# A trunk of eight token tiles on one core: the last pass of three stages in a fixed order, with the next stage's operands made between the finishing steps

## The chip, the core and the metric

One core of a Trainium2 chip runs the whole kernel in one launch. TensorE multiplies, VectorE and ScalarE finish and split results, GpSimd raises one small power per token tile and issues some transfers, and SyncE issues most transfers. The metric is the device time of one launch in microseconds, lower is better. In the profile TensorE is PE, VectorE is DVE, ScalarE is ACT, GpSimd is POOL and SyncE is SP.

## What is computed

1024 tokens of 1024 channels go through two layers, in float32:

```python
for i in range(2):
    hn = rmsnorm(h, norm_mix_g[i])
    h = h + (s5_mixer(hn, ...) if i == 0 else shortconv_mixer(hn, ...))
    h = h + swiglu_ffn(rmsnorm(h, norm_ffn_g[i]), ffn_w_in[i], ffn_w_out[i])
    gate = sigmoid(rmsnorm(h, norm_ple_g[i]) @ ple_w_gate[i])
    h = h + gate * (p[i] @ ple_w_up[i])
return rmsnorm(h, final_norm_g)
```

`s5_mixer` ends in a product with `w_glu` whose one half gates the other; `shortconv_mixer` begins with a product with `conv_w_in` and ends in one with `conv_w_out`; `swiglu_ffn` has a product into 2816 gated channels and one back.

## The kernel before

A float32 product is made of three TensorE passes over a high part and a low part (`split`: ScalarE copies the high part at line 87, VectorE subtracts the rest at line 88; `mm3`: lines 122 to 124). The tokens lie in eight tiles of 128, taken in the order `ORDER` = 0, 4, 1, 5, 2, 6, 3, 7.

The stages alternate between two forms. In the token form (`glu`, `ffn_out`, `ple`, `conv_out`) a tile's matmuls are followed by its finishing operations: a sigmoid where there is a gate, the addition into `h`, and a sum of squares by ScalarE (`square`, line 139). In the channel form (`ffn_in`, `conv_in`) the weights are stationary and all tokens stream past. It uses a scheme that makes a 2 x 2 block product with seven products instead of eight (`block_product`), for which sums and differences of weight blocks (`weights_set`, lines 275 to 283) and of token blocks are needed.

Three times a token stage is followed by a channel stage: `glu` before `ffn_in(0)`, `ple(0)` before `conv_in`, `conv_out` before `ffn_in(1)`. In the last pass over the tiles of these three, `h` becomes complete. Tiles q and q+4 make pair q. `norm_pair(q)` normalizes both (`normed`: the sum of squares at line 146, a power on GpSimd at line 148, the scaling to `xn` at line 173), transposes them on TensorE into four blocks (line 181: `p11`, `p21` from the first tile, `p12`, `p22` from the second), and makes the seven token operands with `put` (a `split`) and the differences T1 to T4 (lines 221 to 232). Operand 0 needs `p11` alone, operand 1 is T2, which needs `p12` and `p22`. `spill` stores `h` by a transfer issued from GpSimd.

Code order is not instruction order here. The framework's scheduler orders the instructions of each engine when the kernel is built, by priority and by its own estimate of times; `first()` raises the priority of the finishing operations and of `normed`. On the chip each engine then runs its list in that order. Buffers come from pools: the temporaries `upt`, `sgg`, `junk`, `b12` and T1 to T4 share five buffers of one tag in the three stages here.

Of the kernel before, what the change touches and what calls it, by code (L numbers as in the profile page):

```python
# [9 lines left out]
F32 = mybir.dt.float32  # L10
F32R = mybir.dt.float32r
# [12 lines left out]
def trunk(  # L24
# [102 lines left out]
    squares = {}  # L127

    def first():
        return tc.high_priority(offset=100)  # L130

    def square(t, cs):
# [5 lines left out]
        ms = squares["ms"][:, t, len(got):len(got) + 1]  # L138
# [3 lines left out]
    def norm_stat(t):  # L142
        ms, *more = squares.pop(t)
        V.tensor_scalar(ms, ms, EPS, None, ALU.add)
# [6 lines left out]
    def t2_tile(name, dt=F32, n=512):  # L151
        return t2.tile([P, n], dt, name=name, tag="t2")
# [54 lines left out]
    def norm_pair(q, gb):  # L207
        t0, t1 = q, q + HT
        halves = 2 if q == HT - 1 else 1
        x0, x1 = normed(t0, gb, halves), normed(t1, gb, halves)  # L210

        def put(c, src):
            split(moving_part(c, 0, q), moving_part(c, 1, q), by_kt(src))

        p11, p12, p22 = transposed(x0, 0), transposed(x1, 0), transposed(x1, 1)
        p21 = transposed(x0, 1, mm)
        put(0, p11)
        b12 = t2_tile("b12")
        A.copy(b12, p12)
        T1 = t2_tile("T1")  # L220
        V.tensor_tensor(T1, b12, p11, ALU.subtract)
        T2 = t2_tile("T2")
        V.tensor_tensor(T2, p22, T1, ALU.subtract)
        put(1, T2)
        put(2, T1)
        put(3, p21)
        T3 = t2_tile("T3")
        V.tensor_tensor(T3, p22, b12, ALU.subtract)
        put(4, T3)
        put(5, p22)  # L230
        T4 = t2_tile("T4")
        V.tensor_tensor(T4, p21, T2, ALU.subtract)
        put(6, T4)

# [23 lines left out]
    def weights_set(src_a, src_b):  # L258
# [15 lines left out]
        s3 = s_tile()  # L274
        V.tensor_tensor(s3, a11, a21, ALU.subtract)
        V.tensor_tensor(a21, a21, a22, ALU.add)
        s2 = s_tile()
        V.tensor_tensor(s2, a21, a11, ALU.subtract)
        ws2 = operand(s2)
        ws1 = operand(a21)  # L280
        w12 = operand(a12)
        ws3 = operand(s3)
        V.tensor_tensor(s2, a12, s2, ALU.subtract)
        return [w11, ws2, ws1, w12, ws3, operand(s2), operand(a22)]
# [131 lines left out]
    def ple(l, units, post):  # L416
# [683 lines left out]
```

## Time and profile before

| What | Value |
|---|---|
| median of 3 runs | 2356.54 us (2355.79 to 2357.86) |
| the profiled execution | 2359.43 us, of which the span is 2357.5 us |
| busy: PE, DVE, ACT, POOL | 2247.0, 1331.9, 765.5, 163.1 us |
| mean granted TensorE clock | 0.981 |
| waits of PE for the scaled tile `xn`, in the whole run | 36.0 us, 5 waits, the longest 10.7 us |
| last pass of `glu`, `ple(0)`, `conv_out` up to the first product of the next stage | 358.5 to 420.6, 1158.1 to 1225.6, 1507.9 to 1571.3 us |

The span runs from the first to the last instruction; 1.9 us of the launch lie outside it. The profiled execution is 2.9 us above the median of the runs. Busy time of PE is modelled for pipelined matmuls, so the waits say more than the 95%. In a timeline row the columns are start, duration, engine, line, operation, output<-inputs with their shapes, count, and in brackets the engine's idle time just before with what ended it.

### The profile page before, as it was taken

How to read it: one execution, taken by the hardware profiler on the slowest of the kernel's cores; microseconds unless marked ns; L12 is line 12 of the kernel's file. 1: busy time of each engine (PE TensorE's matmuls, PEld its weight loads, DVE VectorE, ACT ScalarE, POOL GpSimd, SP SyncE). 2: the span in 40 equal slices, each digit the busy share in tenths (PEclk: the TensorE clock that was granted, in tenths of full speed). 3: DMA queues.
4: the chain of work that ended last, by engine and by line, in shares of the span. 5: the costliest groups of instructions: out<-in, count | busy, mean ns of one | idle time of the engine just before them, and what ended most of it. 6: DMA issues, size and time to landing. Idle time of an engine off the chain costs nothing.

```text
span 2357.5 us, 27090 instructions
## 1 busy us (share of the span) xinstructions
PE 2247.0 (95%) x10253; PEld 1835.7 (78%) x10253; DVE 1331.9 (56%) x2246; ACT 765.5 (32%) x1449; POOL 163.1 (7%) x268
## 2 busy tenths in 40 slices
PE   6888999899999999999979999989999999999998
PEld 4776887788888878878858888768888888788787
DVE  7785326866666642125488776487666666121454
ACT  6554223433333320013343332153333333000232
POOL 2110001000000000000000000010000001000000
PEclk8999999999999999999989999999999999999999
DMA  7555202333333364333232225434333335543333
GB/s 246 141 135 148 69 1 89 105 112 112 111 114 110 107 241 149 118 127 114 70 129 81 90 92 179 159 125 125 108 108 107 111 113 172 212 139 107 108 109 110
DMA packets 212978, 288.87 MB, mean 123 GB/s; under 512 B 21360, under 2 KB 152432, under 8 KB 212848
## 3 DMA queue, kind: packets, MB, share of 16 engines
q1 hardware_dynamic: 191520, 212.63, 29.0%
q0 software_dynamic: 20928, 74.47, 10.2%
q8 instruction: 80, 1.31, 0.2%
q14 instruction: 50, 0.41, 0.1%
q10 hardware_dynamic: 400, 0.04, 0.0%
HBM read 190.93 MB, written 79.69 MB: 115 GB/s over the span
## 4 chain that ended last, share of the span: by engine, by line
PE 85%; DMA 6%; DVE 5%; ACT 1%; SPq 1%; issue 1%; POOL 0%; DVEq 0%; POOLq 0%; ACTq 0%
PE psmm L122 27%; PE psmm L124 27%; PE psmm L123 27%; DMA ch<-hid 2%; PE pstr L181 1%; DMA raw<-in_ffn_w_out_dram 1%; DMA tw<-tmp 1%; DVE W L575 1%; DVE gv L925 1%; DMA h<-hd 1%; DVE tmp L575 1%; DVE ulow L88 1%; DVE uhigh L88 1%; PE pstr L874 0%; DVE raw L575 0%
## 5 line engine op out<-in xcount | busy, mean ns | idle before, releaser
L122 PE MATMUL psmm<-ulow,ws 128*128 128x512 f32 x896 | 351.1, 393 | 1.6 <-ACT s L301 1.6
L123 PE MATMUL psmm<-ulow,ws 128*128 128x512 f32 x896 | 350.6, 391 | 0.0
L124 PE MATMUL psmm<-ulow,ws 128*128 128x512 f32 x896 | 350.4, 391 | 0.0
L124 PE MATMUL psmm<-uhigh,ws 128*128 128x512 f32 x672 | 265.3, 395 | 0.0
L122 PE MATMUL psmm<-uhigh,ws 128*128 128x512 f32 x672 | 265.1, 394 | 0.0
L123 PE MATMUL psmm<-uhigh,ws 128*128 128x512 f32 x672 | 264.9, 394 | 0.0
L360 DVE TENSOR_TENSOR h<-psmm,h 128x512 f32<-128x512 f32 x128 | 88.0, 690 | 276.6 <-PE psmm L124 276.6
L88 DVE TENSOR_TENSOR ws<-raw,ws 128x512 fp32r<-128x512 f32 x224 | 153.6, 688 | 117.8 <-ACT ws L87 117.4
L87 ACT CAST ws<-raw 128x512 fp32r<-128x512 f32 x224 | 137.5, 619 | 213.0 <-PE psmm L124 211.2
L122 PEld LDWEIGHTS psmm<-ulow,ws 128*128 128x128 f32 x896 | 169.4, 189 | 39.5 <-ACT s L301 2.9
L123 PEld LDWEIGHTS psmm<-ulow,ws 128*128 128x128 f32 x896 | 169.4, 189 | 36.2
L124 PEld LDWEIGHTS psmm<-ulow,ws 128*128 128x128 f32 x896 | 169.2, 189 | 36.2
L87 ACT CAST ws<-st 128x512 fp32r<-128x512 f32 x168 | 104.0, 620 | 204.4 <-PE psmm L124 189.5
L123 PEld LDWEIGHTS psmm<-uhigh,ws 128*128 128x128 f32 x672 | 126.1, 188 | 30.3
L124 PEld LDWEIGHTS psmm<-uhigh,ws 128*128 128x128 f32 x672 | 126.1, 188 | 30.3
L122 PEld LDWEIGHTS psmm<-uhigh,ws 128*128 128x128 f32 x672 | 126.1, 188 | 29.1
L323 POOL DMA_DIRECT2D hid<-hs x104 | 78.2, 755 | 903.4 <-DVE hs L88 895.4
L122 PE MATMUL psmm<-ulow,ch 128*128 128x512 f32 x320 | 128.4, 401 | 10.8 <-DMA ch<-hid 10.8
L139 ACT ACTIVATE junk<-h 128x512 bf16<-128x512 f32 (+1 forms) x113 | 64.0, 567 | 204.0 <-DVE h L360 104.0
L87 ACT CAST uhigh<-raw 128x1024 fp32r<-128x1024 f32 x36 | 37.2, 1049 | 278.9 <-PE psmm L124 136.7
L123 PE MATMUL psmm<-ulow,ch 128*128 128x512 f32 x320 | 127.6, 399 | 0.0
L124 PE MATMUL psmm<-ulow,ch 128*128 128x512 f32 x320 | 127.5, 398 | 0.0
(240 smaller groups left out, 4238.5 us busy)
## 6 DMA issues: line engine op xcount, KB each, us to landing
hid<-hs POOLq DMA_DIRECT2D x104, 512.0 KB, 4.3
ch<-hid SPq DMA_DIRECT2D x96, 512.0 KB, 3.7
raw<-in_ffn_w_in_dram SPq DMA_DIRECT2D x88, 512.0 KB, 4.4
raw<-in_ffn_w_out_dram SPq DMA_DIRECT2D x44, 512.0 KB, 3.6
hd<-h POOLq DMA_DIRECT2D x24, 512.0 KB, 3.0
h<-hd SPq DMA_DIRECT2D x24, 512.0 KB, 8.7
raw<-in_conv_w_in_dram SPq DMA_DIRECT2D x24, 512.0 KB, 4.0
up<-ev SPq DMA_DIRECT2D x32, 256.0 KB, 3.2
```

Of the source, the lines that this page charges most:

```text
L87: A.copy(hi, src)
L88: V.tensor_tensor(lo, src, hi.bitcast(F32), ALU.subtract)
L122: PE.matmul(ps, ahi, bhi, start=start, stop=False, skip_group_check=more)
L123: PE.matmul(ps, ahi, blo, start=False, stop=False, skip_group_check=more)
L124: PE.matmul(ps, alo, bhi, start=False, stop=stop, skip_group_check=more)
L139: A.activation(junk[:, cs], h[t][:, cs], AF.Square, scale=1.0 / math.sqrt(D), accum_out=ms)
L181: PE.transpose(pt[:, c * P:(c + 1) * P], xn[:, kt * P:(kt + 1) * P], ident)
L323: nc.gpsimd.dma_start(out=hid[ht // 4][half * HT:(half + 1) * HT, :, ht % 4].rearrange("t p l j -> p t l j"), in_=hs.bitcast(F32))
L360: V.tensor_tensor(h[t][:, cs], ps[nb], h[t][:, cs], ALU.add)
L575: V.tensor_tensor(o, a, b, op)
L925: V.tensor_tensor_scan(gv[:, g, 1:P], dec, sv[:, g, 1:P], 0.0, ALU.mult, ALU.add)
```

## The change

Three things change in the three stages. First, the last pass is written as one loop, `last_pass`, and every TensorE, VectorE and ScalarE instruction in it is chained to the one traced before it on the same engine (`lane`), so that these three engines run in the written order. The written order is, for each tile: its matmuls; with every second tile the 16 transposes of the pair before; then the finishing operations with the pair's steps (`pair_steps`, eleven of them) put in between, one after the addition, one after the squares, one after the sum of squares, and all that are left after `xn`. For the last pair, the first tile is transposed behind the last matmuls, the second when its `xn` is there. Second, the sums and differences of the first weight set of the next stage are held behind the last `xn` on VectorE. Third, the temporaries have their own buffers: `ta`, `tb`, `tc` for the differences, and two buffers instead of five for the rest.

Two things come with it. `conv_out` gets its own loop, in which both halves of a tile are added after all of its matmuls. And in `ple(1)`, which does not use `last_pass`, the two halves of the last tile, which before took one load of `upt`, now each load their own.

```diff
+    def lane():
+        traced = tc.nc.cur_bb.bb.instructions
+        n = len(traced)
+        yield
+        for ins in list(traced[n:]):
+            if ins.engine not in (PE.engine, V.engine, A.engine):
+                continue
+            if ins.engine in lane_ends:
+                tc.add_manual_dep(ins, lane_ends[ins.engine], ..., reason="lane")
+            lane_ends[ins.engine] = ins.name
...
+        return [plain(0, (0, 0)), both(copied, combine("T1", "tb", "b12", (0, 0))), combine("T2", "tc", (1, 1), "T1"),
+                lambda: put(1, tmp["T2"]), lambda: put(2, tmp["T1"]), combine("T4", "tb", (0, 1), "T2"),
+                plain(3, (0, 1)), combine("T3", "tc", (1, 1), "b12"), lambda: put(4, tmp["T3"]), plain(5, (1, 1)),
+                lambda: put(6, tmp["T4"])]
...
+    def last_pass(gb, run):
+        ...
+        with lane():
+            for i, t in enumerate(ORDER):
+                finish, cs = run(t)
+                if i in (2, 4, 6):
+                    q = i // 2 - 1
+                    p = pair_parts(q, {0: xs[q], 1: xs[q + HT]}, [((0, 0), tr), ((1, 0), tr), ((1, 1), tr), ((0, 1), mm)])
+                    todo.extend(pair_steps(q, p))
+                if i == T - 1:
+                    p = pair_parts(HT - 1, {0: xs[HT - 1]}, [((0, 0), mm), ((0, 1), mm)])
+                    steps = pair_steps(HT - 1, p)
+                    todo.insert(0, steps.pop(0))
+                if t in squares:
+                    stat_ahead(t)
+                finish()
+                do(1)
+                square(t, cs)
+                do(1)
+                rs = norm_stat(t, summed=True)
+                do(1)
+                xs[t] = xn = raw_tile(name="xn")
+                halves = 2 if i == T - 1 else 1
+                for c in range(halves):
+                    hs = slice(c * D // halves, (c + 1) * D // halves)
+                    ins = V.scalar_tensor_tensor(xn[:, hs], h[t][:, hs], rs, gb[:, hs], ALU.mult, ALU.mult)
+                spill(t)
+                if i < T - 1:
+                    do(3 if i % 2 else 99)
+            ends[:] = [ins.ins]
+            do(99)
+            p.update(pair_parts(HT - 1, {1: xs[T - 1]}, [((1, 0), tr), ((1, 1), tr)]))
+            todo.extend(steps)
+            do(99)
...
         w11 = operand(a11)
+        with tc.issue_after(ends.pop()) if ends else nullcontext():
             s3 = s_tile()
...
-                upt = t2_tile("upt")
-                nc.sync.dma_start(out=upt, in_=updram[l][:, t, cs])
...
+            def run(t, c0=0, c1=512):
+                hc = slice(nb * 512 + c0, nb * 512 + c1)
+                upt = t2_tile("upt")[:, 0:c1 - c0]
+                nc.sync.dma_start(out=upt, in_=updram[l][:, t, hc])
...
+            if nb == 1 and post is None:
+                last_pass(gb, run)
+                break
```

How the built lists differ is shown at three places, before first and then changed. In a row, `T_...` is a difference, `ws` a weight operand, `ulow` and `uhigh` the room of the token operands, `w_...` the weights of the token stage.

TensorE, last pass of `ple(0)`, around the transposes of the second pair. Before, the eight transposes of its second tile stand 32 matmuls behind the eight of its first:

```order
L124 MATMUL psmm<-w_8491,ulow 128x512
L181 MATMUL pstr<-ident,xn 128x128 x4
L181 MATMUL psmm<-ident,xn 128x128 x4
L122 MATMUL psmm<-w_8380,ulow 128x512
...
L123 MATMUL psmm<-w_8417,ulow 128x512
L181 MATMUL pstr<-ident,xn 128x128 x8
L124 MATMUL psmm<-w_8417,ulow 128x512
```

Changed:

```order
L124 MATMUL psmm<-w_8490,ulow 128x512
L208 MATMUL pstr<-ident,xn 128x128 x12
L208 MATMUL psmm<-ident,xn 128x128 x4
L122 MATMUL psmm<-w_8379,ulow 128x512
L123 MATMUL psmm<-w_8379,ulow 128x512
```

All 16 now stand together, directly behind the matmuls of the pair's following tile, and that tile's successor stands behind them.

VectorE, end of the last pass of `glu`, from the third pair's differences to the last `xn` and a little beyond. Before:

```order
L275 TENSOR_TENSOR st<-raw 128x512
L88 TENSOR_TENSOR ulow<-T_3550,ulow 128x4x128
L502 TENSOR_TENSOR sgg<-psmm,sgg 128x256
L88 TENSOR_TENSOR uhigh<-T_3558,uhigh 128x4x128
L88 TENSOR_TENSOR uhigh<-pstr,uhigh 128x4x128
L88 TENSOR_TENSOR uhigh<-T_3564,uhigh 128x4x128
L276 TENSOR_TENSOR raw<-raw 128x512
L503 TENSOR_TENSOR h<-sgg,h 128x256
L278 TENSOR_TENSOR st<-raw 128x512
L146 TENSOR_TENSOR ms<-ms 128x1
L173 SCALAR_TENSOR_TENSOR xn<-h,rs,gb 128x512 x2
L88 TENSOR_TENSOR ws<-raw,ws 128x512
```

Changed:

```order
L88 TENSOR_TENSOR uhigh<-T_3567,uhigh 128x4x128
L163 TENSOR_SCALAR ms<-ms 128x1
L165 TENSOR_TENSOR ms<-ms 128x1 x2
L595 TENSOR_TENSOR sgg<-psmm,sgg 128x256
L596 TENSOR_TENSOR h<-sgg,h 128x256
L88 TENSOR_TENSOR ulow<-psmm,ulow 128x4x128
L173 TENSOR_TENSOR ms<-ms 128x1
L303 SCALAR_TENSOR_TENSOR xn<-h,rs,gb 128x512 x2
L355 TENSOR_TENSOR st<-raw 128x512
L356 TENSOR_TENSOR raw<-raw 128x512
L88 TENSOR_TENSOR ws<-raw,ws 128x512
L358 TENSOR_TENSOR st<-raw 128x512
```

The three weight sums (lines 275, 276, 278, now 355, 356, 358) moved behind the last `xn`; the finishing of the last tile (lines 595, 596) stands behind the last step of the third pair, as every second tile's does behind its pair. From the last `xn` to the low half of the last pair's operand 1 twelve rows stand in between.

SyncE, the last loads and stores of the kernel, in `ple(1)`. Before:

```order
L424 DMA upt_16880<-up1_97 128x512 [waits DMAHW2_49,DVE_49]
L244 DMA out_0_dram<-xn_16874 128x512 [waits DMAHW3_49,DVE_49]
L244 DMA out_0_dram<-xn_16877 128x512 [waits DMAHW4_49,DVE_49]
L244 DMA out_0_dram<-xn_16947 128x512 [waits DMAHW5_49,DVE_49]
L244 DMA out_0_dram<-xn_16950 128x512 [waits DMAHW6_49,DVE_49]
```

Changed:

```order
L506 DMA upt_16877<-up1_97 128x256 [waits DMAHW2_49,DVE_49]
L323 DMA out_0_dram<-xn_16871 128x512 [waits DMAHW3_49,DVE_49]
L323 DMA out_0_dram<-xn_16874 128x512 [waits DMAHW4_49,DVE_49]
L506 DMA upt_16909<-up1_97 128x256 [waits DMAHW5_49,DVE_49]
L323 DMA out_0_dram<-xn_16946 128x512 [waits DMAHW6_49,DVE_49]
L323 DMA out_0_dram<-xn_16949 128x512 [waits DMAHW7_49,DVE_49]
```

The second half's load has become a transfer of its own, behind two stores, and it waits for VectorE, whose addition of the first half gives its buffer free.

More of the change, by code (lines that the diff above doesn't have):

```diff
@@ new lines, in trunk, with do @@
+    ends = []
+    def last_pass(gb, run):
+        xs, todo = {}, []
+        def do(n):
+            for _ in range(min(n, len(todo))):
+                todo.pop(0)()
+        with lane():
[10 more added lines that the diff above has]
+                if t in squares:
+                    stat_ahead(t)
+                finish()
[17 more added lines that the diff above has]
+            do(99)
+        lane_ends.clear()
@@ L503, in glu @@
                     V.tensor_tensor(h[t][:, cs], sg, h[t][:, cs], ALU.add)
+                return finish, cs
+            if nb == 3:
+                last_pass(gb, run)
+                break
+            for t in ORDER:
+                finish, _ = run(t)
+                with first():
+                    finish()
                     square(t, cs)
-                if nb == 3:
-                    post(t)
     def conv_in(cvq):
```

197 lines of the change are left out of this document (115 added, 82 removed).

## The prediction

> **What bounds the kernel now.** First the chain of waits on the page:
>
> ```profile
> PE 85%; DMA 6%; DVE 5%; ACT 1%; SPq 1%; issue 1%; POOL 0%; DVEq 0%; POOLq 0%; ACTq 0%
> ```
>
> The chain is TensorE (PE) for 85%: what the change can move is time in which PE waits. So next the waits of PE in the three last passes, from the first matmul of the pass to the first product of the next stage (`glu`, `ple(0)`, `conv_out`):
>
> ```profile
> PE pstr L181 <- DVE xn L173: 10.4, 1, 10.4
> PE pstr L181 <- DVE xn L173: 14.8, 3, 10.4
> PE pstr L181 <- DVE xn L173: 10.7, 1, 10.7
> ```
>
> Nearly all that PE waits there is for the scaled tile `xn`, 35.9 us in all. Then the windows of the three passes, and behind them of the next stages' first 168 matmuls (stretch, its length, busy us and instructions of PE, PEld, DVE, ACT and POOL, granted clock, share and GB/s of the DMA):
>
> ```profile
> 358.50:420.60 62.10, 51.68 (x258) 43.42 (x256) 42.84 (x77) 24.40 (x58) 9.07 (x16) 0.94 0.26 94
> 1158.10:1225.60 67.50, 52.66 (x258) 43.62 (x256) 47.33 (x77) 26.93 (x56) 9.10 (x17) 0.90 0.31 109
> 1507.90:1571.30 63.40, 52.69 (x257) 43.44 (x256) 46.44 (x82) 26.02 (x60) 9.64 (x16) 0.94 0.38 133
> 420.60:461.90 41.30, 40.62 (x170) 32.53 (x169) 36.51 (x61) 20.24 (x35) 1.56 (x2) 0.96 0.35 101
> 1225.60:1266.40 40.80, 40.13 (x168) 32.34 (x167) 32.56 (x52) 16.65 (x29) 0.44 (x2) 0.95 0.27 78
> 1571.30:1611.50 40.20, 39.98 (x170) 32.29 (x169) 36.56 (x61) 20.84 (x38) 1.55 (x2) 0.97 0.39 118
> ```
>
> PE is busy for 52 of 62 to 67 us. VectorE (DVE) has 43 to 47 us of work in a pass, so it is not full, but it is not far from full either. The timeline of PE at the end of the pass of `ple(0)`:
>
> ```profile
> 1195.32 1.04 PE L181 MATMUL pstr<-ident,xn 128*128 128x128 f32 x8
> 1196.11 0.48 PE L124 MATMUL psmm<-w,ulow 128*128 128x512 f32 x1
> ...
> 1200.64 0.48 PE L122 MATMUL psmm<-w,ulow 128*128 128x512 f32 x1
> ...
> 1205.97 0.39 PE L124 MATMUL psmm<-w,ulow 128*128 128x512 f32 x1
> 1207.80 1.09 PE L181 MATMUL pstr<-ident,xn 128*128 128x128 f32 x8 [1.45 <-DVE xn L173]
> ...
> 1223.97 1.97 PE L181 MATMUL pstr<-ident,xn 128*128 128x128 f32 x8 [10.39 <-DVE xn L173]
> 1225.59 0.78 PE L122 MATMUL psmm<-ulow,ws 128*128 128x512 f32 x1
> ```
>
> Eight transposes take 0.79 us (1195.32 to 1196.11). The 24 matmuls of one tile run from 1200.64 to 1205.97, 5.33 us for 23 steps at nearly one step in 0.227 us, so 5.44 us a tile. PE is done at 1206.36 and gets the last `xn` at 1223.97, 17.6 us later. Why so late, DVE tells:
>
> ```profile
> 1218.33 0.68 DVE L433 TENSOR_TENSOR upt<-psmm,upt 128x512 f32<-128x512 f32 x1
> ...
> 1223.17 1.41 DVE L173 SCALAR_TENSOR_TENSOR xn<-h,rs,gb 128x512 f32<-128x512 f32 x2 [0.75 <-POOL cvp L527]
> ```
>
> The last tile's matmuls ended at 1206.36, but the product with its gate started at 1218.33, behind operands of the third pair; from there to its `xn` it is 4.8 us. Much of the wait is thus order, not work.
>
> **The change, part by part.** *Length of the fixed order.* It puts a tile's finishing operations ahead of the pair's steps, but it also puts the next tile's finishing behind the last of them, on DVE and on ScalarE (ACT), and the transposes of a pair directly behind the tile that follows it. What counts then is the cycle of DVE over two tiles against that of PE. Latencies from the timelines, of ACT:
>
> ```profile
> 1196.01 0.59 ACT L219 COPY b<-pstr 128x512 f32<-128x512 f32 x1 [1.73 <-PE pstr L181]
> 1197.35 0.62 ACT L87 CAST ulow<-T 128x512 fp32r<-128x512 f32 x1 [0.75 <-DVE T L221]
> ...
> 1204.80 0.63 ACT L139 ACTIVATE junk<-h 128x512 bf16<-128x512 f32 x1 [2.67 <-DVE h L435]
> ...
> 1206.39 0.58 ACT L432 ACTIVATE psmm<-psmm 128x512 f32<-128x512 f32 x1 [0.87 <-PE psmm L124]
> ```
>
> and of DVE:
>
> ```profile
> 1196.63 0.69 DVE L221 TENSOR_TENSOR T<-b,pstr 128x512 f32<-128x512 f32 x1 [0.83 <-ACT b L219]
> 1197.42 0.69 DVE L223 TENSOR_TENSOR T<-pstr,T 128x512 f32<-128x512 f32 x1
> 1198.03 0.68 DVE L228 TENSOR_TENSOR T<-pstr,b 128x512 f32<-128x512 f32 x1
> ...
> 1204.02 0.68 DVE L435 TENSOR_TENSOR h<-upt,h 128x512 f32<-128x512 f32 x1
> 1205.55 0.16 DVE L146 TENSOR_TENSOR ms<-ms 128x1 f32<-128x1 f32 x1 [0.85 <-ACT junk L139]
> 1206.46 1.28 DVE L173 SCALAR_TENSOR_TENSOR xn<-h,rs,gb 128x1024 f32<-128x1024 f32 x1 [0.75 <-POOL rs L148]
> 1207.67 0.68 DVE L433 TENSOR_TENSOR upt<-psmm,upt 128x512 f32<-128x512 f32 x1
> 1208.38 0.69 DVE L435 TENSOR_TENSOR h<-upt,h 128x512 f32<-128x512 f32 x1
> ```
>
> From start to start: ACT copy to DVE 0.62 (1196.01 to 1196.63); difference to a difference that needs it 0.79 (1196.63 to 1197.42); difference to its ACT copy 0.72 (1196.63 to 1197.35); neighbours without dependence 0.60 (1197.42 to 1198.03); product to sum 0.71 (1207.67 to 1208.38); sum to squares 0.78 (1204.02 to 1204.80); squares to sum of squares 0.75 (to 1205.55); from there over POOL to `xn` 0.91 (to 1206.46); `xn` occupies DVE for 1.21 (to 1207.67) and reaches PE after 1.34 (the transposes at 1207.80). Matmul end to sigmoid is 0.03 (1206.36 to 1206.39). The squares hold ACT for 0.63.
>
> In the fixed order, counted from an even tile's product at 0: sum 0.71, low half of operand 0 1.31, squares 1.49, copy of `p12` 2.12, T1 2.74, sum of squares 3.34, T2 3.53, `xn` 4.25, low halves of operands 1 and 2 at 5.46 and 6.06, T4 6.66. The ACT copy of `p21` is ordered behind T4, so operand 3's low half is at 6.66 + 0.72 + 0.62 = 8.00; T3 8.60, its operand by the same two steps 9.94, the last two low halves 10.54 and 11.14. Only now the odd tile: product 11.85 (a small sum of 0.1 lies before), sum 12.56, squares 13.34, sum of squares 14.09, `xn` 15.00, its transposes 16.34, and the next even product 16.3. DVE works 11.8 us of the 16.3 (11 steps and 4 finishing operations at 0.60, two `xn` at 1.21, four small ones at 0.1); 4.5 us it waits for ACT and POOL, with nothing left to put in for the odd tile. PE needs two tiles and 16 transposes: 2 x 5.44 + 1.58 = 12.46 us. The order is 3.8 us longer than PE's work, in each cycle.
>
> *`ple(0)`.* First cycle: the even product is at 0.03 + 0.62 after PE's third tile; the second pair's transposes could start 0.65 + 16.34 = 17.0 after it, PE is there after 12.5: a wait of 4.5. Second: 3.85. End: the last `xn` is made in halves, so PE gets its first at 15.00 + 0.80 after the product (0.80 by 1223.17 to 1223.97); the product lies 0.05 before the third pair's transposes, and PE has behind their start 1.58 + 5.44 + 0.79 of work: a wait of 7.95. In all 16.3 instead of 14.8: **+1.5 us**.
>
> *`glu`.* Its finishing operations are half as wide:
>
> ```profile
> 402.73 0.42 DVE L502 TENSOR_TENSOR sgg<-psmm,sgg 128x256 f32<-128x256 f32 x1
> 403.18 0.42 DVE L503 TENSOR_TENSOR h<-sgg,h 128x256 f32<-128x256 f32 x1
> ...
> 403.70 0.42 ACT L139 ACTIVATE junk<-h 128x256 bf16<-128x256 f32 x1 [1.10 <-DVE h L503]
> ```
>
> Product to sum 0.45 and sum to squares 0.52 save 0.26 each. The squares of half the width I take 0.21 shorter, an estimate from their durations of 0.63 and 0.42. That is 1.46 in a cycle; three small dependent sums a tile, for four quarters of squares, give back some 0.35 each. Cycle 15.55; waits 3.4, 3.1 and 6.85, in all 13.35 instead of 10.4: **+2.9**.
>
> *`conv_out`.* No sigmoid, and the first half's addition can run early: the first wait is 1.3 shorter, 3.2; the cycle of two sums and squares is as long as `ple`'s: 3.85, 7.95. In all 15.0 instead of 10.7: **+4.3**. The pauses in the windows of about 2 us for loads of `ch` lie ahead of this pass and stay.
>
> *Weight sums behind `xn`.* A long pause leaves PE with a slow clock; the third number from the end is the granted clock:
>
> ```profile
> 2014.60:2018.10 3.50, 0.05 (x2) 0.03 (x1) 0.00 (x0) 0.00 (x0) 0.00 (x0) 0.95 1.02 407
> 2018.10:2021.20 3.10, 3.10 (x7) 2.45 (x8) 0.00 (x0) 0.54 (x1) 0.00 (x0) 0.51 0.69 276
> ...
> 1477.60:1479.90 2.30, 0.10 (x2) 0.11 (x2) 0.82 (x2) 0.00 (x0) 0.00 (x0) 1.00 0.93 331
> ```
>
> The first product needs operand 0 and the high and low halves of one weight block, which are there in time; the second needs the low half of the last pair's operand 1, before which stand twelve DVE rows: 12 x 0.60 + 0.72 = 7.9 us behind the end of `xn`. PE gets there at about 6.2 (transposes until 1.1, as the rows at 1223.97 and 1225.59 show for a slow clock, then twelve matmuls at some 0.43, as 7 took 3.10). That is a wait of about 1.5 in each stage. The three sums at 0.60 that were done while PE waited are now a backlog of 1.8; in the windows above DVE is busy for 36.5 of 41.3 and 36.6 of 40.2 us behind `glu` and `conv_out`, so there I let 1.5 of it reach PE, behind `ple` (32.6 of 40.8) nothing. 1.5 x 3 + 1.5 x 2 = 7.5, less the 0.7 that PE waited there before and does not twice: **+7**. Bounds: 0, if the slow clock covers it all, and 3.5 in each stage, 10.5.
>
> *The last tile of `ple(1)`.*
>
> ```profile
> 2349.37 0.41 DVE L433 TENSOR_TENSOR upt<-psmm,upt 128x256 f32<-128x256 f32 x1
> 2350.43 0.42 DVE L433 TENSOR_TENSOR upt<-psmm,upt 128x256 f32<-128x256 f32 x1 [0.65 <-ACT psmm L432]
> ```
>
> Before, the second half's product followed the first's after 1.06. Now it must wait for the first sum (some 0.45 behind the product, its end 0.42 later, as in `glu`), and then for a load. The loads of `upt` here are twice as large and land so, from their issue:
>
> ```profile
> DMA to landing us min/median/max: 2.6/2.7/7.2
> ```
>
> For the half I take 2.3 us, an estimate between half of the 2.6, below which I see no reason to go, and the 2.7. 2349.37 + 0.87 + 0.05 + 2.3 = 2352.6 instead of 2350.43; behind it lies one sum, not two, so some 0.3 comes back: **+1.9**, at the kernel's end, where nothing hides it. By the bounds it is 0.9 to 2.3.
>
> *At nothing:* `spill` now goes tile by tile; its issue on POOL precedes the power by the time of the squares. Two buffers for `upt` and `junk`: an `upt` can be loaded as soon as the sum before it is done, 11 us ahead of the next even tile and 4 of an odd one, and landing takes 2.7 at the median.
>
> Sum: 1.5 + 2.9 + 4.3 + 7 + 1.9 = 17.6 us. The profiled execution, 2359.4, becomes 2377.0; the median of 2356.5 becomes **2374 us**, 0.75% slower.
>
> **Rivals.** *Faster.* If the 4.5 us that DVE waits in a cycle were mostly covered, the two waits amid a pass would vanish and only the last tile's own chain would remain: 0.03 + 0.62 + 0.71 + 0.78 + 0.75 + 0.91 + 0.80 less 0.79 of transposes, 3.8 us a pass. That saves 35.9 - 11.4 = 24.5; with 7 and 1.9 on the other side the time is 2341. For it speaks that DVE's work, 11.8, is below 12.46; against it that each of the waits is a row above, and that the code gives the odd tile nothing to fill them with. A cycle shorter by 1 us shortens three waits in three stages, 9 us: break-even is at a cycle of about 14.3, the whole gain at 12.5.
>
> *Slower still.* The clock rows above: a pause of 3.5 us cost half the clock for the 3.1 us behind it; in one of 2.3 us it stayed at 1.00. The waits of 3.1 to 4.5 us amid the passes may do the same. I set this to 0, since DVE, not PE, then bounds the cycle and has 3.8 us to spare on PE. If PE's lost time lay on the path, some 2.2 us (half of 4 to 5 us) six times would be added: 2374 + 13 = 2387. [...]
>
> *No change.* The weight term at its lower bound and a cycle shorter by 1 us leave 17.6 - 7 - 9 = 1.6 us: 2358. That the change is not in the program is excluded by the built order.
>
> **How the numbers follow.** Forecast 0.68, slower still 0.12, no change 0.07, faster 0.13. About 0.2% or 4.7 us is what a measurement of this kernel can tell from no change, so slower has 0.80, same 0.07, faster 0.13. The forecast's own range is 2364 (weights at 0, tail at 1) to 2382 (weights at 10.5, 0.1 us more for each of the cycle's handovers). The range to hold 8 in 10 takes in part of each neighbour: 2360 to 2387.
>
> **What would show it.** In the changed profile PE should wait for `xn` three times in each last pass, about 3 to 4.5, 3 to 4 and 7 to 8 us, with the finishing of the odd tile right behind the last low half of a pair; the first product should be followed by a wait for a low half at line 88; and the load of the last half tile should end the wait of its product. The prediction is wrong if the two early waits are missing or under 1 us, which would mean that ACT and POOL answer faster between DVE's rows than I counted.

## The result and the profile after

The changed kernel takes 2379.9 us (median of 4 runs, 2377.6 to 2381.8) against 2357.2 us before; the ratio is 1.0102, 95% interval 1.0088 to 1.0117. It is slower by 1.0%; the medians lie 22.7 us apart. (Each ratio here is to runs of the kernel before taken alongside, so it is not quite the quotient of the medians in the table.) The profiled execution took 2381.8 us with a span of 2380.0.

The windows of the three last passes, and then of the first 168 matmuls of the next stages, in the changed kernel:

```profile
355.30:420.20 64.90, 53.47 (x257) 44.88 (x257) 44.03 (x92) 21.89 (x54) 9.06 (x16) 0.95 0.27 89
1158.70:1226.60 67.90, 54.74 (x257) 45.84 (x256) 46.73 (x78) 25.77 (x54) 9.10 (x17) 0.92 0.36 116
1516.20:1583.60 67.40, 54.63 (x257) 44.81 (x256) 46.01 (x78) 25.35 (x59) 9.02 (x16) 0.93 0.40 133
420.20:464.80 44.60, 41.07 (x170) 32.47 (x169) 39.24 (x64) 22.03 (x39) 1.56 (x2) 0.96 0.30 88
1226.60:1269.20 42.60, 40.40 (x169) 32.08 (x168) 35.83 (x57) 17.46 (x31) 1.43 (x2) 0.97 0.26 75
1583.60:1630.40 46.80, 44.39 (x170) 34.50 (x169) 38.77 (x64) 22.07 (x39) 1.55 (x2) 0.89 0.29 85
```

The passes grew by 2.8, 0.4 and 4.0 us. The starts of the next stages, counted to the start of the 169th matmul (the windows end up to 0.5 us short of it), grew by 3.2, 1.5 and 6.6. VectorE's work in a pass is within 1.2 us of what it was; its place in time changed. TensorE's waits for `xn` in the passes of `glu`, `ple(0)` and `conv_out`, from its timeline:

```profile
387.62 1.09 PE L208 MATMUL pstr<-ident,xn 128*128 128x128 f32 x8 [2.66 <-DVE ms L163]
403.36 1.97 PE L208 MATMUL pstr<-ident,xn 128*128 128x128 f32 x8 [2.86 <-DVE xn L303]
418.66 1.73 PE L208 MATMUL pstr<-ident,xn 128*128 128x128 f32 x7 [5.91 <-DVE xn L303]
...
1192.38 1.97 PE L208 MATMUL pstr<-ident,xn 128*128 128x128 f32 x8 [4.11 <-DVE xn L303]
1209.03 1.09 PE L208 MATMUL pstr<-ident,xn 128*128 128x128 f32 x8 [0.94 <-DVE ms L163]
1225.04 1.94 PE L208 MATMUL pstr<-ident,xn 128*128 128x128 f32 x8 [8.12 <-DVE xn L303]
...
1548.86 1.09 PE L208 MATMUL pstr<-ident,xn 128*128 128x128 f32 x8 [2.28 <-DVE xn L303]
1565.43 1.09 PE L208 MATMUL pstr<-ident,xn 128*128 128x128 f32 x8 [1.88 <-DVE xn L303]
1582.01 1.94 PE L208 MATMUL pstr<-ident,xn 128*128 128x128 f32 x8 [8.61 <-DVE xn L303]
```

Before, one wait stood at the end of the pass in `glu` and `conv_out`; now three stand in each pass, two of them in its middle. (Two rows name `ms` at line 163, which VectorE runs right behind `xn`; the transposes read `xn`.) The longest wait of TensorE behind the first product of each of the next stages; the first two are for the low half of the last pair's operand 1, the third for the high half of a weight operand:

```profile
427.92 0.50 PE L123 MATMUL psmm<-ulow,ws 128*128 128x512 f32 x1 [2.40 <-DVE ulow L88]
...
1234.03 0.50 PE L123 MATMUL psmm<-ulow,ws 128*128 128x512 f32 x1 [2.08 <-DVE ulow L88]
...
1591.52 0.80 PE L122 MATMUL psmm<-ulow,ws 128*128 128x512 f32 x1 [1.98 <-ACT ws L87]
```

And VectorE's two products of the last tile of `ple(1)`, now 4.15 us apart instead of 1.06:

```profile
2369.12 0.42 DVE L514 TENSOR_TENSOR upt<-psmm,upt 128x256 f32<-128x256 f32 x1
...
2373.27 0.42 DVE L514 TENSOR_TENSOR upt<-psmm,upt 128x256 f32<-128x256 f32 x1 [2.48 <-DMA upt<-up]
```

One place that the prediction did not have is the first pass of `conv_out`, 53.7 us instead of 48.0, with one longer wait for `ch`.

### The profile page after: what moved, and what is told of

It is laid out like the page before. It is cut to its first block, busy times and chain, and to the rows that moved or that the text cites. A ratio compares the mean times of both kernels' runs of the same rounds, so it can differ in the third digit from the quotient of the medians.

```text
span 2380.0 us, 27138 instructions
## 1 busy us (share of the span) xinstructions
PE 2259.7 (95%) x10253; PEld 1846.0 (78%) x10253; DVE 1335.8 (56%) x2243; ACT 764.1 (32%) x1449; POOL 162.9 (7%) x268
## 5 line engine op out<-in xcount | busy, mean ns | idle before, releaser
L440 DVE TENSOR_TENSOR h<-psmm,h 128x512 f32<-128x512 f32 x96 | 66.1, 691 | 247.4 <-PE psmm L124 247.4
L123 PE MATMUL psmm<-uhigh,ch 128*128 128x512 f32 x320 | 126.7, 396 | 0.5 <-DVE uhigh L88 0.5
## 6 DMA issues: line engine op xcount, KB each, us to landing
h<-hd SPq DMA_DIRECT2D x24, 512.0 KB, 11.3
```

Source lines behind the costliest of these rows:

```text
L123: PE.matmul(ps, ahi, blo, start=False, stop=False, skip_group_check=more)
L440: V.tensor_tensor(h[t][:, cs], ps[nb], h[t][:, cs], ALU.add)
```

## The experiments

All kernels together, each stretch read from that kernel's own profiled execution. "Passes" is the sum of the three last passes, "starts" the sum of the three stretches behind them, each from its first product to the start of the 169th matmul (the expectations below count up to 0.7 us less), "`conv_out` first" that stage's first pass, "end" the time from the first matmul of the last pass of `ple(1)` to the end of the span.

| Kernel | median us | ratio to before (95%) | passes | starts | `conv_out` first | end |
|---|---|---|---|---|---|---|
| before | 2357.2 | 1 | 193.0 | 123.0 | 48.0 | 51.6 |
| changed | 2379.9 | 1.0102 (1.0088 to 1.0117) | 200.2 | 134.4 | 53.7 | 54.3 |
| no_chain | 2344.8 | 0.9958 (0.9943 to 0.9972) | 173.3 | 130.8 | 47.9 | 54.0 |
| chain_dve_only | 2387.7 | 1.0132 (1.0117 to 1.0148) | 211.6 | 135.1 | 47.6 | 53.3 |
| chain_pe_one_load | 2341.2 | 0.9934 (0.9921 to 0.9946) | 173.9 | 130.1 | 47.6 | 51.6 |
| spread_steps | 2360.9 | 1.0022 (1.0012 to 1.0032) | 176.9 | 141.6 | 51.0 | 53.2 |
| no_hold | 2384.5 | 1.0124 (1.0107 to 1.0141) | 204.8 | 138.8 | 48.0 | 53.4 |
| hold_later | 2372.7 | 1.0068 (1.0054 to 1.0082) | 200.1 | 126.9 | 53.3 | 53.3 |
| one_load | 2380.1 | 1.0103 (1.0086 to 1.0120) | 200.1 | 135.1 | 54.1 | 51.6 |
| h_place | 2376.0 | 1.0087 (1.0069 to 1.0106) | 200.1 | 133.5 | 49.2 | 53.3 |
| chain_pe_warm | 2344.3 | 0.9945 (0.9932 to 0.9957) | 175.8 | 127.4 | 47.4 | 51.6 |
| all_chains_filled | 2348.8 | 0.9966 (0.9955 to 0.9977) | 178.0 | 127.0 | 53.9 | 51.6 |
| chain_pe_hold_later | 2342.2 | 0.9936 (0.9921 to 0.9951) | 173.9 | 128.9 | 46.7 | 51.6 |

**no_chain.** The dependences are left out:

```diff
-            if ins.engine in lane_ends:
+            if False:
                 tc.add_manual_dep(ins, lane_ends[ins.engine], ..., reason="lane")
```

> The changed kernel without the chain of dependences: the code is written in the same order, but the scheduler may place the instructions of TensorE, VectorE and ScalarE where it likes. Changed kernel: the three last passes take 64.9, 67.9 and 67.4 us (together 200.2, before 193.0), the first 168 matmuls of the next stages 44.6, 42.6 and 46.8 us. Theory A (the fixed order is the cost: VectorE waits 4.5 us in each cycle for ScalarE and GpSimd with nothing else to put in): the two waits for xn amid each pass fall under 1 us, the passes together drop by at least 12 us, to 188 or less, and the time falls to 2365 us or below. Theory B (the cost lies in how the steps are written, the 16 transposes of a pair in one piece and eight steps behind an even tile's xn, chain or no chain): the waits amid the passes stay at 2 us and more, the passes stay at 196 us or more together, and the time stays at 2374 or above.

2344.8 us, 35 us below the changed kernel and 0.4% below the one before. The windows of the three passes:

```profile
355.40:412.80 57.40, 51.85 (x258) 43.42 (x256) 39.17 (x70) 22.76 (x54) 9.06 (x16) 0.97 0.28 101
1151.30:1209.40 58.10, 52.40 (x258) 43.20 (x256) 43.28 (x70) 26.22 (x54) 9.10 (x17) 0.96 0.41 136
1493.20:1551.10 57.90, 53.13 (x257) 43.32 (x255) 41.94 (x74) 26.16 (x59) 9.33 (x16) 0.96 0.45 155
```

TensorE's busy time falls by 1.5 to 2.3 us a pass, the rest of the gain is its waits: the passes take 26.9 us less than with the chain. In `ple(0)` VectorE multiplies by the gate at 1181.72, 1187.96 and 1194.24:

```profile
1181.72 0.69 DVE L514 TENSOR_TENSOR upt<-psmm,upt 128x512 f32<-128x512 f32 x1 [0.72 <-DMA upt<-up]
1187.96 0.69 DVE L514 TENSOR_TENSOR upt<-psmm,upt 128x512 f32<-128x512 f32 x1
1194.24 0.68 DVE L514 TENSOR_TENSOR upt<-psmm,upt 128x512 f32<-128x512 f32 x1
```

Two tiles take 12.52 us, which is TensorE's 12.46. The same rows of the changed kernel:

```profile
1192.49 0.69 DVE L514 TENSOR_TENSOR upt<-psmm,upt 128x512 f32<-128x512 f32 x1
1204.52 0.68 DVE L514 TENSOR_TENSOR upt<-psmm,upt 128x512 f32<-128x512 f32 x1
1208.95 0.68 DVE L514 TENSOR_TENSOR upt<-psmm,upt 128x512 f32<-128x512 f32 x1
```

There the odd tile's product comes 12.03 us behind the even one's and the cycle is 16.46 us. Theory A holds: the change without its chain is a gain, and the chain turns it into a loss. How much of that gain comes from the order in which the code is written and how much from the temporaries' own buffers was not separated.

**chain_dve_only** and **chain_pe_one_load.** Which engine's chain costs?

```diff
-            if ins.engine not in (PE.engine, V.engine, A.engine):
+            if ins.engine not in (V.engine,):        # chain_dve_only
+            if ins.engine not in (PE.engine,):       # chain_pe_one_load
```

The second also has the one load of **one_load**, below.

> The changed kernel with the chain on VectorE alone; TensorE and ScalarE are placed by the scheduler. With no chain the three last passes together took 173.3 us, with all three chains 200.2. Theory A (VectorE's fixed order is the cost: it waits at each handover to ScalarE and GpSimd with work standing behind that could go): the passes stay at 195 us or more, the two waits for xn amid the passes stay, and the time is 2370 or more. Theory B (the cost is TensorE's order, all 16 transposes of a pair in one piece behind the following tile): the passes fall below 180 us and the time to 2355 or less.

> The changed kernel with the chain on TensorE alone, and one load of upt for the last tile of ple(1). Theory A (VectorE's fixed order is the cost): the passes are as short as without any chain, 171 to 177 us together, the stretch from the product of the last tile's first half to the end is 8.1 us instead of 10.9, and the time is 2337 to 2343, below the kernel without a chain (2344.8) and the kernel before. Theory B (TensorE's order, the transposes of a pair in one piece, is the cost): the passes stay at 190 us or more, the waits amid them come back, and the time is 2360 or more.

VectorE's order alone costs all of it and more (2387.7 us, passes 211.6). TensorE's order alone costs nothing (2341.2 us, passes 173.9). The 16 transposes in one piece are harmless; what hurts is the fixed order of VectorE, the engine that answers two others. A chain on ScalarE alone was not run. With VectorE chained and ScalarE free the passes are even longer than with all three chained; why was not followed up.

**spread_steps.** The chain stays, its content changes: the eleven steps of a pair reach into the odd tile, whose handovers had nothing in them.

```diff
-                    do(3 if i % 2 else 99)
+                    do(99 if i % 2 else 3)
```

> The changed kernel with the chain kept, but a pair's eleven steps divided over two tiles: three amid the finishing of the even tile and three behind its xn, three amid the finishing of the odd tile, and the last two behind its xn (before: eleven by the end of the even tile, none for the odd one). Theory A (the handovers in which VectorE idles set the cycle, and an order that fills them shortens it): VectorE works 11.8 us in a cycle and PE 12.46, so the two waits for xn amid the passes fall under 1.5 us each, the three passes lose 12 to 24 us (200.2 to 176 to 188), the next stages' first 168 matmuls grow by up to 6 us, as two more steps of the third pair lie behind the last xn, and the time falls to 2362 to 2372. Theory B (a fixed order as such costs, whatever it is, because each handover it fixes is waited for): the waits only move, the passes stay above 195 us together, and the time stays within 4 us of 2380.

The passes fall by 23.4 us to 176.9, as theory A has it, and the waits amid them to 1.2 us or less. The starts grow by 7.2 (it put them at up to 6): three of the third pair's steps now lie behind the last `xn` (the expectation counted two); the time, 2360.9, ends 1.1 us below its range.

**no_hold** and **hold_later.** The weight sums are not held at all, or held two VectorE rows longer than the change does.

```diff
-        with tc.issue_after(ends.pop()) if ends else nullcontext():
+        with nullcontext():                            # no_hold
...
             todo.extend(steps)
+            do(2)                                      # hold_later
+            ends[:] = [[x for x in tc.nc.cur_bb.bb.instructions if x.engine == V.engine][-1]]
             do(99)
```

> The changed kernel with the weight sums no longer held behind the last xn, the chain kept. Theory A (the prediction's term: the hold makes PE wait for the second pair of operands of the next stage and leaves VectorE a backlog): the first 168 matmuls of the next stages (134.0 us for the three, before 122.3) lose 6 to 11 us, the wait for a low half at line 88 behind the first product goes, the time falls to 2369 to 2374. Theory B (the last pair's steps are late by themselves, since the whole third pair and the last tile's finish stand ahead of them, and the sums of weights only change places with them): the three stretches stay within 3 us of 134.0 or grow, and the time stays at 2377 or above.

> The changed kernel, chains as they are, with the weight sums held two DVE rows further, behind the last pair's second difference T2 instead of behind the last xn. With the hold at xn the first 168 matmuls of the next stages take 134.0 us together, without any hold 138.6, before the change 122.3. Theory A (the weights' rows that stand ahead of the last pair's operand 1 are what PE waits for): the waits at line 123 for a low half, 2.4, 2.1 and 2.0 us, go, the three stretches fall by 5 to 8 us, the passes stay, and the time falls to 2371 to 2375. Theory B (VectorE's total work behind the last xn is the bound, whatever its order): the wait only moves to the weight operands of the second or third product, the stretches stay within 2.5 us of 134.0, and the time stays at 2377 or above.

Without the hold it is 4.6 us slower, as theory B had it: the passes grow by 4.5 us and the starts by 4.4. VectorE's timeline before the last `xn` of `conv_out` shows one reason; the sums of lines 355, 356 and 358 stand amid the last tile's finishing:

```profile
1583.05 0.69 DVE L355 TENSOR_TENSOR st<-raw 128x512 f32<-128x512 f32 x1
...
1583.85 0.69 DVE L356 TENSOR_TENSOR raw<-raw 128x512 f32<-128x512 f32 x1
...
1585.12 0.69 DVE L358 TENSOR_TENSOR st<-raw 128x512 f32<-128x512 f32 x1
1586.27 1.41 DVE L303 SCALAR_TENSOR_TENSOR xn<-h,rs,gb 128x512 f32<-128x512 f32 x2 [0.46 <-POOL rs L175]
```

They no longer stand behind `xn`, but `xn` itself is late. And other weight rows have taken their places: in `glu` eleven VectorE rows lie between the last `xn` and T2, ten of them for weights, with a wait of 1.80 us for a weight load among them, and TensorE waits longer for operand 1 than with the hold:

```profile
431.26 1.74 PE L122 MATMUL psmm<-ulow,ws 128*128 128x512 f32 x3 [5.06 <-ACT ulow L87]
```

With the longer hold, whose `ends` is then the instruction of T2, the starts lose 7.5 us, and the time 7.2:

```profile
419.40:461.50 42.10, 40.78 (x170) 32.48 (x169) 39.20 (x65) 22.14 (x39) 1.56 (x2) 0.96 0.37 113
1223.20:1265.50 42.30, 40.22 (x170) 32.11 (x169) 38.03 (x59) 17.16 (x30) 0.70 (x3) 0.98 0.27 75
1579.10:1621.20 42.10, 40.91 (x169) 32.75 (x168) 39.26 (x65) 22.20 (x39) 1.56 (x2) 0.95 0.37 113
```

So most of what the starts had gained in length came from weight rows ahead of the last pair's operand 1, and not from a full VectorE (behind `glu` it does 39.2 us of work in 42.1, as much as in the changed kernel's 44.6). But the three stages differ. Of the 7.5 us, 4.7 are behind `conv_out`, where the changed kernel's clock had fallen a second time (granted clock 0.50 for 6.8 us, below), 2.3 behind `glu`, and only 0.5 behind `ple(0)`. There theory B is right: the wait of 2.08 us for the operand is gone, and this one, for the high half of a weight operand, stands in its place, and another of 0.5 for the low half of one:

```profile
PE psmm L122 <- ACT ws L87: 1.6, 1, 1.6
```

In all 3.9 us more than before the change are left. In the prediction's words, the weight rows among the twelve are the greater part of the cost; the hold as such is not, against the same chain without it.

**one_load.** The two halves of the last tile of `ple(1)` share a load again; `load_up` takes a buffer of all 512 columns and starts its load.

```diff
-                upt = t2_tile("upt")[:, 0:c1 - c0]
-                nc.sync.dma_start(out=upt, in_=updram[l][:, t, hc])
+                upt = (load_up(t) if up is None else up)[:, c0:c1]
...
+                up = load_up(t) if last else None
```

> The changed kernel, but the two halves of the last tile of ple(1) share one load of upt as in the kernel before. Theory A (the second half's own load, which waits for the first half's sum, is the whole of the longer tail): the product of the second half follows that of the first after 1.1 us instead of 4.15, the stretch from the first half's product to the end is 8.1 us instead of 10.9, and the time falls by 2.8, to 2377. Theory B (the order of the last tile's sums and squares changed as well): the stretch stays above 9.5 us, and the time falls by less than 1.5.

```profile
2368.28 0.42 DVE L518 TENSOR_TENSOR upt<-psmm,upt 128x256 f32<-128x256 f32 x1
2369.34 0.42 DVE L518 TENSOR_TENSOR upt<-psmm,upt 128x256 f32<-128x256 f32 x1 [0.64 <-ACT psmm L517]
```

The products are 1.06 us apart again, as theory A has it, and the end takes 51.6 us as before the change instead of 54.3. The median does not show it: the four runs lie from 2373.8 to 2382.1, wider than the 2.7 us. The mechanism is shown by the rows, its size in the time is not.

**h_place.** In the changed kernel, one_load, hold_later and all_chains_filled the first pass of `conv_out` takes 53 to 54 us (51.0 in spread_steps), in the kernels without the full chain, or without the hold, about 48. The changed kernel's TensorE wait there, and SyncE's timeline:

```profile
PE psmm L122 <- DMA ch<-hid: 6.6, 1, 6.6
```

```profile
1454.61 13.31 SPq L653 DMA_DIRECT2D h<-hd  x5
...
1466.18 1.75 SPq L653 DMA_DIRECT2D h<-hd  x4
```

VectorE's timeline at the same moment:

```profile
1466.18 0.69 DVE L397 TENSOR_TENSOR s<-psmm,s 128x512 f32<-128x512 f32 x1 [0.86 <-PE psmm L124]
```

Of the five loads the first went out at 1454.61 and the next four only at 1466.18, when TensorE had ended the last product of `conv_in` (its sum starts at that moment); the loads of `ch` stand behind them in the same queue. The edit gives the second tile's buffer to the tile that is loaded last:

```diff
-        h_tiles()
+        h_tiles([{HT: T - 1, T - 1: HT}.get(t, t) for t in ORDER] if name == "c" else ORDER)
```

> The changed kernel with one edit: in conv_out the buffers of h for tiles 4 and 7 change places, so that the buffer under the last weight operand of conv_in belongs to the tile that is loaded last, not second. The first pass of conv_out took 53.7 us in the changed kernel, 54.1 with one load and 53.3 with the later hold; 48.0 before, and 47.6 to 48.0 without a hold, without a chain, and with one chain alone. Theory A (the second load of h waits 11.6 us for the last product of conv_in, because its buffer lies where that product's weights lie, and holds up the loads of ch behind it on SyncE; without that, 7.9 us): the first pass of conv_out takes 47.5 to 48.5 us, the pause of 6.6 us for ch falls to 2 or less, all other stages stay, and the time falls by 5 to 6, to 2374 to 2375. Theory B (the loads there collide on the DMA engines in any case, by when the stage starts): the pass stays above 52 us and the time within 2 us of 2380.

```profile
1454.70 9.67 SPq L653 DMA_DIRECT2D h<-hd  x5
```

```profile
PE psmm L122 <- DMA ch<-hid: 2.6, 2, 2.4
```

The pass falls to 49.2 us, 4.5 of the 5.7, the longest wait to 2.4 and the median by 3.9: theory A, each a little short of what it expected. The loads were late because of the place of a buffer, in a pass whose products the change leaves as they were. In the kernel before, the waiting loads went out one product earlier, when VectorE took up the last but one of `conv_in`:

```profile
1459.89 1.74 SPq L348 DMA_DIRECT2D h<-hd  x3
...
1459.90 0.69 DVE L315 TENSOR_TENSOR u<-psmm,u 128x512 f32<-128x512 f32 x1 [1.50 <-PE psmm L124]
```

In no_hold it is the same (both at 1472.46, line 395), and h_place puts them back there. So, by these times, the second tile's buffer lies where the weights of the last product lie in the changed kernel, and in the others where those of the product before it do. Why the buffers came to lie so was not looked into.

**chain_pe_warm.** Forty unused products fill TensorE's wait at the end of the pass, to keep its clock up.

```diff
+            warm = psum()
+            for _ in range(40):
+                PE.matmul(warm[:, 0:P], identn, identn, start=True, stop=True)
             p.update(pair_parts(HT - 1, {1: xs[T - 1]}, [((1, 0), tr), ((1, 1), tr)]))
```

> The kernel of chain_pe_one_load, and in each of the three stages 40 more 128x128 products into a bank that nobody reads, issued between the first transposes of the last pair and the last eight, where TensorE waits 4 to 5 us for xn. Theory A (the half clock behind that pause is time on the path): the granted clock behind the passes stays at 1.0, the first 168 matmuls of the next stages take 1.5 to 3 us less each (130.8 together without a chain), and the time falls by 4 to 9 us against chain_pe_one_load. Theory B (VectorE, which makes the last pair's operands and the weights', bounds these stretches, and a faster TensorE only waits): the sum of the three stretches stays within 2 us, waits for low halves at line 88 grow by what the clock gives, and the time stays within 2 us. If the products outlast the wait, the passes grow by up to 1 us each.

Neither theory holds throughout. The windows of the three starts, and of a stretch in the start behind `ple(0)`:

```profile
412.00:454.20 42.20, 39.62 (x168) 31.16 (x169) 37.59 (x63) 22.04 (x38) 1.56 (x2) 1.00 0.32 93
1212.40:1254.40 42.00, 40.76 (x169) 32.26 (x170) 35.34 (x56) 17.61 (x30) 0.83 (x2) 0.97 0.27 76
1552.30:1595.10 42.80, 40.46 (x168) 32.27 (x168) 38.61 (x64) 21.87 (x38) 1.55 (x2) 0.96 0.31 90
1208.40:1215.20 6.80, 4.76 (x15) 3.68 (x16) 5.76 (x10) 3.10 (x6) 0.61 (x2) 0.50 0.45 152
```

Behind `glu` the clock stays at 1.00 and the start is 2.4 us shorter (42.4 against 44.7). Behind `ple(0)` 2.5 us of the wait were left, and the clock fell all the same, 0.8 us after the end of the forty products (1207.6): 0.50 over the 6.8 us of the last row. The starts gain 2.7 us in all, the passes lose 1.9, and the stretches from the first start to `ple(0)` and from the third to `ple(1)`, which hold the two `ffn_out` stages, came out 3.7 and 2.5 us longer in this execution, though the edit does not touch them. At one place in the first of them the clock was at half for 6.8 us where chain_pe_one_load has 3.4 (rows in the last section). The median is 3.1 us above chain_pe_one_load. There is nothing to win here with this filler; how much the clock alone is worth stays open.

**all_chains_filled** and **chain_pe_hold_later.** The parts put together: spread_steps, one_load and the weights held until T1, with all chains; and chain_pe_one_load with the weights held until T1.

> All three chains of the changed kernel kept, with the steps of a pair divided over two tiles (three behind the even tile's xn), the weight sums held until the last pair's first difference instead of its xn, and one load of upt for the last tile of ple(1). Parts measured: the divided steps took 23 us from the passes and gave 7.6 back in the next stages; the later hold took 7.5 us from those; the tail was worth 2.7. Theory A (what the order leaves idle costs, not that it is fixed; the three parts add up): the passes stay at 175 to 180 us together, the next stages' first 168 matmuls fall from 141.6 to 126 to 134, and the time is 2343 to 2352, below the kernel before. Theory B (VectorE is full behind the last xn, as two more steps of the third pair lie there, so the later hold gains nothing): those stretches stay above 138 us, and the time is 2355 or more.

> The kernel of chain_pe_one_load (2341.2 us) with the weight sums held until the last pair's first difference instead of the last xn. Theory A (the weights' rows ahead of the last pair's operand 1 cost here too): the next stages' first 168 matmuls fall from 129.9 to 126 to 128 us, and the time to 2337 to 2339. Theory B (without a chain on VectorE the scheduler already puts the rows in the order in which they are needed): the stretches stay within 1.5 us and the time within 2 us of 2341.

All three chains with a fuller order: 2348.8 us, 0.34% faster than before the change, although its first pass of `conv_out` still has the 53.9 us. It is theory A: most of what the chain cost came from what its order left idle, not from its being fixed. Not all: against chain_pe_hold_later, which leaves VectorE and ScalarE to the scheduler and does not divide the steps, 6.6 us remain (passes 178.0 against 173.9, the first pass of `conv_out` 53.9 against 46.7, starts 127.0 against 128.9). With VectorE left free the longer hold brings nothing (2342.2 against 2341.2 us): theory B.

## Why the prediction was right, and where it was off

Forecast 2374 us (range 2360 to 2387), measured 2379.9. Against the profiled execution the sum was +17.6; the two profiled spans differ by 22.5. The mechanism, a cycle of VectorE that is longer than TensorE's work, was right; that the total came as near as it did is partly luck (last item). By its terms:

- **The cycle of 16.3 us in `ple`** measured 16.46, with the odd product at 12.03 where the count gave 11.85. It carried the passes of `ple(0)`, `glu` and `conv_out`: +1.5, +2.9, +4.3 forecast, +0.4, +2.8, +4.0 measured. That 4.5 us of it are idle handovers, and not work, is what spread_steps and no_chain show.
- **The two waits amid each pass** (`ple(0)`, `glu`, `conv_out`) were forecast as 4.5 and 3.85, 3.4 and 3.1, 3.2 and 3.85; measured were 4.11 and 0.94, 2.66 and 2.86, 2.28 and 1.88. The 0.94 is under the 1 us that the prediction named as a sign of being wrong, though the cycle there is as long as counted. The second ones of `ple(0)` and `conv_out` are short because TensorE had lost the time already:

```profile
1191.50:1198.40 6.90, 6.01 (x21) 5.27 (x21) 6.00 (x10) 2.33 (x5) 1.13 (x2) 0.51 0.52 191
1549.90:1553.30 3.40, 3.40 (x12) 2.83 (x11) 2.39 (x6) 1.89 (x6) 1.13 (x2) 0.51 0.66 267
```

  The granted clock is 0.51 in both, and TensorE's products start 0.43 us apart there (1195.43 and 1195.86) and 0.23 from 1198.40 on. Half the clock for the 6.0 and 3.4 us in which TensorE worked is 3.0 and 1.7 us lost, an estimate from these rows, and with 0.94 and 1.88 that makes 3.9 and 3.6, near the forecast waits. This is the rival "slower still": the clock did fall, and it was hidden behind VectorE, as the prediction argued when it set that term to 0: the cycle of `ple(0)` came to 16.46 us, near the count, with the 3.0 us lost in it. hold_later fits this: there the two waits of `conv_out` were 2.33 and 3.45 us instead of 2.28 and 1.88, and the pass took 67.3 us against 67.4. The 4 to 5 us of slow clock that the rival reckons with were the author's estimate, which no run shows; measured in the changed kernel were 0.51 for 6.9 us behind the wait of 4.11 us, 0.53 for 3.4 us behind that of 2.86 (403.30 to 406.70), 0.51 for 3.4 us behind that of 2.28, and 1.00 behind the other three.
- **Weight sums behind `xn`** was the term of the sum that was mis-sized: +7 forecast, bounds 0 to 10.5, measured +11.3 (from 123.0 to 134.4), beyond its bounds. The waits of about 1.5 were 2.40, 2.08 and 1.98. In `glu` the operand was there 8.75 us behind the end of `xn` (419.17 to 427.92), where the count gave 7.9; 0.47 of it VectorE waited for a weight load:

```profile
424.77 0.69 DVE L355 TENSOR_TENSOR st<-raw 128x512 f32<-128x512 f32 x1 [0.47 <-DMA raw<-in_ffn_w_in_dram]
...
427.19 0.68 DVE L88 TENSOR_TENSOR ulow<-T,ulow 128x512 fp32r<-128x512 f32 x1
```

  And behind `conv_out`, in the third of the waits, the clock fell a second time, for 6.8 us (granted clock 0.50):

```profile
1590.90:1597.70 6.80, 6.18 (x15) 4.79 (x16) 5.12 (x10) 3.23 (x7) 0.00 (x0) 0.50 0.52 155
```

  TensorE worked for 6.2 of them, so by the same estimate 3.1 us were lost, which no term had; with it the stretch grew by 6.6. The direction, and rows of weights ahead of operand 1 as the greater part of the cost, are what hold_later showed; the 3.9 us that it leaves were not followed up.
- **The last tile of `ple(1)`**: +1.9 forecast, bounds 0.9 to 2.3, the end grew by 2.7. The wait for the load is there (2.48 us), and one_load undoes it. The distance of the products came to 4.15 where the count gave 3.23: the load, estimated at 2.3 us, was issued at 2370.02 and waited for until 2373.27.
- **A term at nothing that was not nothing**: the first pass of `conv_out`, +5.8. The prediction followed the loads of `upt` and the spills, not where the next stages' buffers come to lie; h_place gives 4.5 us of it back.
- The rest of the program, outside all these stretches, was 4.6 us shorter in the profiled execution, 3.2 of them before the first of the three passes. The rests of the other eleven kernels lie 1.2 to 7.9 us below the one of before as well, so it may be the execution of before that was long there; that is not shown. This and the +5.8 nearly cancel, which is luck: without the -4.6 the sum would have been off by 9.5 us and not by 4.9.

The rival "faster" (two waits vanish, 3.8 us remain at the end, 2341) failed for this kernel on its own condition, a cycle of 14.3 us or less. In a kernel that meets the condition, no_chain with its 12.52, nearly all of it came true: end waits of 5.4, 4.7 and 3.8 us, no pause of 1 us amid a pass, and 2344.8 us.

## What to carry to other kernels

Before an order is fixed by hand on an engine that hands results back and forth with others, lay out one cycle from start to start, and look for handovers with no work behind them. Here VectorE idled at them for 4.5 of 16.3 us by the count, although it was busy for only 44 to 47 of the 65 to 68 us of a pass, and what cured it was to spread the independent steps over all handovers (passes 200.2 to 176.9 us) or to leave that engine to the scheduler (173.9). A chain on TensorE alone cost nothing here (2341.2 us). After any reordering, look also at the stages behind it: one buffer that came to lie over the weights of the last product held up a queue of loads a stage later, and moving it took 4.5 us off that stage's first pass.

## What the runs showed of the hardware

In these runs the clock did not follow the length of one pause. In the changed kernel, behind the wait of 2.66 us in `glu` it stayed at 1.00 (the window below), behind that of 2.28 us in `conv_out` it fell to 0.51 (the window from 1549.90 above):

```profile
387.62:391.00 3.38, 3.38 (x21) 3.04 (x22) 2.73 (x9) 0.98 (x3) 0.74 (x2) 1.00 0.23 93
```

Nor did its cost: behind nearly equal pauses for `ch` at the same place in the program, 3.74 us in chain_pe_one_load and 3.78 in chain_pe_warm, half the clock lasted 3.4 us in the one and 6.8 in the other. The windows of these two:

```profile
864.90:868.30 3.40, 3.40 (x10) 2.62 (x9) 0.00 (x0) 1.04 (x1) 0.00 (x0) 0.50 0.31 124
```

```profile
860.30:867.10 6.80, 5.79 (x14) 4.53 (x15) 0.26 (x1) 1.05 (x1) 0.00 (x0) 0.50 0.50 198
```

TensorE worked at half clock for 3.40 us in the one and for 5.79 in the other, so 1.2 us more were lost in chain_pe_warm, an estimate from these rows, for no cause that they show in the stage's own instructions.

Nor did the busy share just before tell the cases apart. In the changed kernel TensorE was busy for 0.56 of the 3.22 us before 387.62, and the clock stayed up; it was busy for 2.00 of the 3.40 us before 1590.90, and the clock fell to 0.50:

```profile
384.40:387.62 3.22, 0.56 (x5) 0.32 (x4) 1.89 (x4) 1.25 (x4) 1.14 (x2) 1.00 0.40 163
1587.50:1590.90 3.40, 2.00 (x7) 0.84 (x5) 3.02 (x5) 3.05 (x7) 0.00 (x0) 1.00 0.00 0
```

What decides when the clock falls, and for how long, is not shown.
